# Four changes around the joint of gated mixing, attention and output projection in a one-layer encoder kernel on Trainium2

## The chip, the cores and the metric

The kernel runs on one core of one Trainium2 chip. The metric is the device time of one execution in microseconds (us): the median of three runs. The core has five engines with an instruction queue each: TensorE (PE, matmuls), VectorE (DVE), ScalarE (ACT), GpSimd (POOL) and SyncE (SP), which here issues nearly all DMAs. Each queue is worked off in program order; across engines, semaphores hold an instruction back until its inputs are there and its output buffer is free.

## The reference, cut to what matters

One pre-norm encoder layer on 2048 tokens of width 1024, in float32:

```python
xn = rms_norm(x, mix_norm_g)
q, k, v, f_logit, z = split(xn @ w_in)            # 8 heads of 64; z has 2 x 512 columns
c = cumsum(log_sigmoid(f_logit + b_f))
attn = softmax(causal(q k^T / 8 + c[t] - c[s])) @ v
zu, zv = split(gelu(z)); zv = layer_norm(zv, ln_g, ln_b)
sgu = zu * (masked w_s @ zv + b_s)                # within chunks of 128 tokens, 8 groups of 64
merged = concat(rms_norm(attn, g_a), rms_norm(sgu, g_s))
x = x + merged @ w_out
gate, up = split(rms_norm(x, ffn_norm_g) @ w_gate_up)
x = x + (silu(gate) * up) @ w_down
out = rms_norm(x, final_norm_g)
```

## The kernel before

Every float32 factor is split into a high part in a shorter matmul type and a low part, the rest (names ending in h and l); a product is three matmuls, high by high, high by low, low by high. Making the two parts takes an ACT cast (line 103) and a DVE subtraction (line 108).

The program goes through the input projection (to 356 us of the span), the attention, the output projection (to 1185 us), the up half of the FFN (to 2045 us), the down half (to 2470 us) and a tail. The attention runs 320 steps: for each of 8 heads and each of 4 chunks j of 512 queries, the 4j+4 key blocks of 128 that the mask leaves. A step is two score matmuls into st (lines 627 and 628), an exp by ACT into Pt (line 630), the ACT cast to Ph and the DVE subtraction to Pl, on diagonal blocks two GpSimd selects that put zeros above the diagonal (line 639), and, two steps later, three pv matmuls (lines 646 to 648). After a chunk's last block ACT copies the sums and the denominators out (nd, line 654) and SP stores them (SD, AT); for the last head the denominators of all heads come back as sr, are inverted by DVE, and are stored as RD.

Other work is threaded into the steps by counters on the step number n. The gate path has 8 units of 2 token tiles. A unit is `z_proj` (64 steps of projections, line 696, then copies, a Gelu over 2048 columns on ACT, line 710, the layer norm on DVE with the small power rlr on GpSimd, and the parts zvh and zvl) and `z_mix` (24 small matmuls, line 735; products with DVE, line 740; a sum of squares on ACT, line 746; the power rsr on GpSimd; 8 transposes, line 753; copies sT). The mix of unit i runs inside the projection of unit i+1. The counter goes by n/ZEND, so the gate path is spread over the first 293 steps; projections end at n = 279. From there `out_weights` makes the parts of w_out: 8 loads of 512 KB into two buffers of `xap`, and 16 pairs of a scaled ACT copy (line 835, high part, R0h, R2h, R5h, R6h) and a DVE subtraction (line 836, low part). After its second half has been read, a buffer is loaded again, two loads ahead. At ZEND + 7 the output projection joins the steps: `out_prep` loads a token tile (ST, AT, and the inverse denominators RD), normalises and splits it, line 930 multiplies, and `out_done` stores the sum and the transposed tile XT for the FFN. Token tiles go 0 to 15, FFN halves of 8 tiles in the same order.

The instructions' order on each engine is set by a scheduler that keeps the program's dependencies; it is fixed when the program is built. DMAs on SP are in its order too. Keys (D, C) and values (V) of a head and chunk are loaded two units ahead (`prep`, `load_keys`).

## Time and profile before

| what | us |
|---|---|
| median of three runs | 2479.53 |
| lowest and highest run | 2474.86, 2481.61 |
| the profiled execution | 2481.27 |
| its span, first to last instruction | 2479.6 |
| PE busy | 2415.8 (97%) |
| DVE busy | 1568.5 (63%) |
| ACT busy | 1054.0 (43%) |
| POOL busy | 596.7 (24%) |

All rows below are of the profiled execution, with times from the start of its span. "Busy" of PE is modelled: matmuls are pipelined, so the durations of two that follow each other overlap. The clock that the throttle grants to PE is given as a share of 2.4 GHz.

### The profile page before, as it was taken

What the parts mean: (1) busy time and instruction counts of PE and PEld (TensorE: products, weight loads), DVE (VectorE), ACT (ScalarE), POOL (GpSimd) and SP (SyncE); (2) the same over time, 40 slices, a digit from 0 to 9 for tenths busy, and PEclk for the clock granted to TensorE, in tenths of its full rate; (3) what the DMA queues carried; (4) which work ended last, traced back from release to release, by engine and by line L of the source; (5) the groups of instructions that cost most, each with busy time, mean ns of one, the idle gap of its engine ahead of it and who ended that gap; (6) DMA issues with size and microseconds to landing.
All of it is one profiled execution on the core that took longest, in us unless ns stands there. A gap on an engine that the chain in (4) does not pass through costs nothing. (4 is left out here: it accounts for less than half of the span.)

```text
span 2479.6 us, 31430 instructions
## 1 busy us (share of the span) xinstructions
PE 2415.8 (97%) x10729; PEld 1930.5 (78%) x10729; DVE 1568.5 (63%) x2551; ACT 1054.0 (43%) x1787; POOL 596.7 (24%) x666
## 2 busy tenths in 40 slices
PE   7999999999999989999999999999999999999997
PEld 5777777788787767877888888788888877888876
DVE  4457485666666656466555555875556586696887
ACT  5322226677777776344332322433233242332333
POOL 1000010111111112122232232332323234453441
PEclk9999999999999989999999999999999999999999
DMA  9776565444444337765423223332232244455453
GB/s 312 256 240 199 165 201 144 134 114 127 118 112 115 96 111 194 222 201 166 136 68 94 80 82 94 111 111 77 79 95 74 85 130 168 170 187 192 146 181 144
DMA packets 356263, 355.31 MB, mean 143 GB/s; under 512 B 55364, under 2 KB 276356, under 8 KB 355080
## 3 DMA queue, kind: packets, MB, share of 16 engines
q1 hardware_dynamic: 353800, 344.91, 45.0%
q0 software_dynamic: 2304, 8.39, 1.1%
q8 instruction: 86, 1.41, 0.2%
q14 instruction: 73, 0.60, 0.1%
HBM read 236.50 MB, written 116.72 MB: 142 GB/s over the span
## 5 line engine op out<-in xcount | busy, mean ns | idle before, releaser
L103 ACT CAST wh<-raw 128x512 fp32r<-128x512 f32 (+2 forms) x500 | 309.6, 624 | 796.5 <-PE pp L1300 657.4
L108 DVE TENSOR_TENSOR wl<-raw,wh 128x512 fp32r<-128x512 f32 (+2 forms) x500 | 374.6, 758 | 116.2 <-ACT wh L103 115.8
L1031 POOL TENSOR_TENSOR raw<-raw 128x512 f32<-128x512 f32 (+1 forms) x124 | 165.4, 1335 | 552.5 <-DMA raw<-in_w_gu_dram 365.1
L108 DVE TENSOR_TENSOR Pl<-Pt,Ph 128x512 fp32r<-128x512 f32 (+1 forms) x320 | 194.5, 615 | 158.8 <-ACT Ph L103 155.0
L630 ACT ACTIVATE Pt<-st 128x512 f32<-128x512 f32 (+1 forms) x320 | 167.9, 534 | 149.9 <-PE st L628 148.6
L696 PE MATMUL z<-wh,xz 128*128 128x512 f32 x512 | 199.5, 397 | 0.0
L103 ACT CAST Ph<-Pt 128x512 fp32r<-128x512 f32 (+1 forms) x320 | 176.2, 557 | 22.6 <-PE pv L647 6.2
L1031 DVE TENSOR_TENSOR raw<-raw,raw 128x512 f32<-128x512 f32 (+1 forms) x112 | 133.2, 1191 | 73.2 <-POOL raw L1031 69.3
L337 DVE TENSOR_REDUCE mx<-mx_ps 128x1 f32<-128x512 f32 x192 | 130.8, 686 | 37.6 <-PE mx_ps L335 35.1
L646 PE MATMUL pv<-Ph,V 128*128 128x512 f32 (+2 forms) x320 | 123.6, 387 | 11.7 <-POOL Ph L639 8.8
L639 POOL TENSOR_SCALAR_AFFINE_SELECT Ph<-Ph 128x128 fp32r<-128x128 f32 x128 | 44.2, 345 | 374.7 <-DVE Pl L108 255.0
L627 PE MATMUL st<-A,D 74*128 74x512 f32 (+1 forms) x320 | 120.7, 378 | 3.8 <-ACT Pt L630 3.8
L335 PE MATMUL mx_ps<-D,A 66*128 66x512 f32 (+2 forms) x320 | 118.5, 382 | 4.8 <-DVE mx L337 3.7
L648 PE MATMUL pv<-Pl,V 128*128 128x512 f32 (+1 forms) x320 | 119.7, 375 | 1.0 <-DVE Pl L108 0.4
L628 PE MATMUL st<-B,C 128*128 128x512 f32 (+1 forms) x320 | 118.3, 370 | 0.0
L647 PE MATMUL pv<-Ph,V 128*64 128x512 f32 (+1 forms) x320 | 116.4, 364 | 0.0
L696 PEld LDWEIGHTS z<-wh,xz 128*128 128x128 f32 x512 | 96.7, 189 | 19.2
L1300 PE MATMUL pp<-R2h,wh 128*128 128x512 f32 x264 | 105.4, 399 | 5.7 <-ACT u L1089 5.7
L1300 PE MATMUL pp<-R3h,wl 128*128 128x512 f32 x264 | 105.0, 398 | 2.6 <-DVE wl L108 2.6
L1300 PE MATMUL pp<-R1h,wl 128*128 128x512 f32 x264 | 104.6, 396 | 0.7 <-DVE wl L108 0.7
L1300 PE MATMUL pp<-R2h,wl 128*128 128x512 f32 x264 | 104.9, 397 | 0.2 <-DVE wl L108 0.2
L1146 POOL TENSOR_TENSOR hT<-hT 128x512 f32<-128x512 f32 x44 | 74.4, 1693 | 127.3 <-DVE hT L1145 104.2
(335 smaller groups left out, 6294.1 us busy)
## 6 DMA issues: line engine op xcount, KB each, us to landing
raw<-in_w_gu_dram SPq DMA_DIRECT2D x88, 512.0 KB
HD<-hT SPq DMA_DIRECT2D x44, 512.0 KB
xz<-XS SPq DMA_DIRECT2D x32, 512.0 KB
D<-KH SPq DMA_DIRECT2D x112, 128.0 KB
XA<-xa SPq DMA_DIRECT2D x27, 512.0 KB
xa<-XA SPq DMA_DIRECT2D x24, 512.0 KB
raw<-HD SPq DMA_DIRECT2D x24, 512.0 KB
xb<-XA SPq DMA_DIRECT2D x24, 512.0 KB
```

The lines of the kernel that those rows point to most:

```text
L103: nc.scalar.copy(o, i)
L108: eng.tensor_tensor(o, i, f(h), ALU.subtract)
L335: nc.tensor.matmul(pm[:, 0:n], lhs, Dt[0 : lhs.shape[0], 0:n], start=True, stop=True)
L337: nc.vector.tensor_reduce(mx[:, a, s : s + 1], pm, AX.X, ALU.max)
L627: nc.tensor.matmul(st[:, off:], Dt[:, b * P : (b + 1) * P], A[:, off:], start=True, stop=False)
L628: nc.tensor.matmul(st[:, off:], C[:, b * P : (b + 1) * P], B[:, off:], start=False, stop=True)
L630: nc.scalar.activation(Pt[:, off:], st[:, off:], AF.Exp)
L646: nc.tensor.matmul(pv[:, off:], V[:, 0:P], Ph[:, off:], start=kb == 0, stop=False)
L648: nc.tensor.matmul(pv[:, off:], V[:, 0:P], Pl[:, off:], start=False, stop=kb == 4 * j + 3)
L696: nc.tensor.matmul(pz, xz[:, a, k, :], w[b][:, k, :], start=n == 0, stop=n == 3 * KT - 1)
L1031: (nc.vector if e == "v" else nc.gpsimd).tensor_tensor(o, a, b, op)
L1300: nc.tensor.matmul(pm, a[:, k, :], b[:, k, :], start=on is None and k == 0 and e == 0, stop=k == it.kh - 1 and e == 2, skip_group_check=n ...
```

## The change

There are four edits.

- The last head's query chunks run in the order 3, 2, 1, 0 instead of 0 to 3. Its keys and values, which chunk 3 needs whole, are loaded chunk by chunk, chunk 0 in `prep` and 1 to 3 during head 6's last chunk. The output projection takes the token tiles as 12 to 15, 8 to 11, 4 to 7, 0 to 3, and the FFN takes its second half of tiles first.
- In the gate path, the mix of unit 6 no longer runs inside the projection of unit 7 but behind it, in one piece ("on" makes the step loop take it without a break), and that of unit 7 after it. ZEND goes from 293 to 299, so the projections end at n = 285.
- The high parts of w_out are made by GpSimd (`tensor_scalar_mul`) instead of ACT.
- In the input projection of the last chunk, behind the values of its second token tile, an Exp of 4 columns is added on ACT, ahead of the first exp of the attention, which loads the exp table before.

```diff
-ZEND = 293
+ZEND = 299
...
+        if xc.c == NCH - 1 and tt == 1:
+
+            nc.scalar.activation(T(p1, [P, 4], F32, "r1a"), f(v[:, 0, 0:4]), AF.Exp)
...
-        load_keys(h, j)
+        if h < H - 1 or j == NCH - 1:
+            load_keys(h, j if h < H - 1 else 0)
...
-    units = [(h, j) for h in range(H) for j in range(NCH)]
+
+    units = [(h, j) for h in range(H) for j in (range(NCH) if h < H - 1 else range(NCH - 1, -1, -1))]
+    tiles = [4 * j + t for j in range(NCH - 1, -1, -1) for t in range(4)]
...
-                if n >= 8 and n % 2 == 0:
+                if i < H - 1 and n >= 8 and n % 2 == 0:
                     next(mix, None)
                 yield
             for _ in mix:
-                yield
+                yield "on"
             mix = z_mix(i, *res[0])
...
-            nc.scalar.activation(h_, raw[n][:, i, :], AF.Copy, scale=g)
+            nc.gpsimd.tensor_scalar_mul(h_, raw[n][:, i, :], g)
             nc.vector.scalar_tensor_tensor(l_, raw[n][:, i, :], g, f(h_), ALU.mult, ALU.subtract)
...
-        gens = [out_prep(t, o[t]) for t in range(NB)]
+        gens = [out_prep(tiles[t], o[t]) for t in range(NB)]
...
-                        posts.append(out_done(t, o[t]["x"]))
+                        posts.append(out_done(tiles[t], o[t]["x"]))
...
-                next(zg, None)
+                while next(zg, None) == "on":
+                    pass
...
             pv_of(h, j, kb)
+            if (h, j) == (H - 2, NCH - 1) and kb in (3, 7, 11):
+                load_keys(H - 1, (kb + 1) // 4)
...
-                ld(t, XT[s - 1][i])
+                ld(t, XT[2 - s][i])
...
-    sets = ([[Up(half, fi) for fi in range(NF)] for half in range(2)]
+    sets = ([[Up(half, fi) for fi in range(NF)] for half in (1, 0)]
```

Line numbers behind the added lines go up: line 835 becomes 841, 836 becomes 842, 735 becomes 739, 740 becomes 744, 696 becomes 700, 639 becomes 643, 646 to 648 become 650 to 652.

On PE, behind the last projection matmul into z, the order before was (pv of the last diagonal blocks of a chunk, and the next scores):

```order
L696 MATMUL z_9669<-wh_3191,xz_9495 128x512
L646 MATMUL pv_9528<-Ph_9774,V_882_3326 128x384
L647 MATMUL pv_9528<-Ph_9774,V_882_3326 64x384
L648 MATMUL pv_9528<-Pl_9776,V_882_3326 128x384
L627 MATMUL st_9850<-A_9257,D_9252 128x512
L628 MATMUL st_9850<-B_9260,C_9249 128x512
L646 MATMUL pv_9528<-Ph_9791,V_882_3326 128x256
```

and in the changed kernel it is, up to the first of the 24 mix matmuls of unit 6:

```order
L700 MATMUL z_9712<-wh_3191,xz_9555 128x512
L650 MATMUL pv_9768<-Ph_9820,V_884_3329 128x512
L651 MATMUL pv_9768<-Ph_9820,V_884_3329 64x512
L652 MATMUL pv_9768<-Pl_9822,V_884_3329 128x512
L631 MATMUL st_9874<-A_9244,D_9583 128x512
L632 MATMUL st_9874<-B_9247,C_9580 128x512
L739 MATMUL z_9907<-zvh_9187,wsth_3324 128x128
```

The mix matmuls of unit 6 have moved behind the projections of unit 7, all 24 in one run, and the blocks around them are off the diagonal.

On POOL, at the same place, the order before (selects Ph and Pl of the diagonal blocks, and rlr, the power of the last unit's layer norm) was:

```order
L639 AFFINE_SELECT Pl_9793<-Pl_9793 128x128
L639 AFFINE_SELECT Ph_9808<-Ph_9808 128x128
L639 AFFINE_SELECT Pl_9810<-Pl_9810 128x128
L639 AFFINE_SELECT Ph_9855<-Ph_9855 128x128
L639 AFFINE_SELECT Pl_9857<-Pl_9857 128x128
L154 TENSOR_TENSOR rlr_9874<-rla_9872,mhalf_201 128x2
L639 AFFINE_SELECT Ph_9897<-Ph_9897 128x128
```

and after (R0h, R2h, R5h are high parts of w_out out of the loaded xa; rsr is the power of the mix's norm):

```order
L841 TENSOR_SCALAR R0h_9991<-xa_9872,onc_9868 128x512 x2
L841 TENSOR_SCALAR R2h_10067<-xa_10012,onc_9868 128x512 x2
L154 TENSOR_TENSOR rlr_9896<-rla_9894,mhalf_201 128x2
L841 TENSOR_SCALAR R2h_10067<-xa_10045,onc_9868 128x512 x2
L154 TENSOR_TENSOR rsr_9948<-rsa_9946,mhalf_201 128x2
L643 AFFINE_SELECT Ph_10076<-Ph_10076 128x128
L643 AFFINE_SELECT Pl_10078<-Pl_10078 128x128
L643 AFFINE_SELECT Ph_10097<-Ph_10097 128x128
L643 AFFINE_SELECT Pl_10099<-Pl_10099 128x128
L841 TENSOR_SCALAR R5h_10159<-xa_10090,onc_9868 128x512 x2
L841 TENSOR_SCALAR R5h_10159<-xa_10130,onc_9868 128x512 x2
L643 AFFINE_SELECT Ph_10116<-Ph_10116 128x128
```

The high parts, which POOL did not do before, now stand ahead of rlr and ahead of selects.

On DVE, at the third and fourth pair of loads (low parts R2l, R5l; Pl; products of the mix into sg), before:

```order
L836 SCALAR_TENSOR_TENSOR R2l_10010<-xa_9987,onc_9828,R2h_10009 128x512
L108 TENSOR_TENSOR Pl_10062<-Pt_10058,Ph_10060 128x512
L108 TENSOR_TENSOR Pl_10085<-Pt_10081,Ph_10083 128x384
L662 RECIPROCAL sr_10048<-sr_10048 128x32
L740 SCALAR_TENSOR_TENSOR sg_9884<-z_10002,bsc_3497,zr_9124 128x2x64 x2
L836 SCALAR_TENSOR_TENSOR R5l_10106<-xa_10034,onc_9828,R5h_10105 128x512
L108 TENSOR_TENSOR Pl_10116<-Pt_10112,Ph_10114 128x256
```

and after:

```order
L842 SCALAR_TENSOR_TENSOR R2l_10068<-xa_10045,onc_9868,R2h_10067 128x512
L744 SCALAR_TENSOR_TENSOR sg_9968<-z_9969,bsc_3499,zr_9208 128x2x64 x4
L842 SCALAR_TENSOR_TENSOR R5l_10160<-xa_10090,onc_9868,R5h_10159 128x512 x2
L108 TENSOR_TENSOR Pl_10118<-Pt_10114,Ph_10116 128x256
L744 SCALAR_TENSOR_TENSOR sg_9968<-z_10060,bsc_3499,zr_9208 128x2x64 x4
L108 TENSOR_TENSOR Pl_10139<-Pt_10135,Ph_10137 128x128
L842 SCALAR_TENSOR_TENSOR R5l_10160<-xa_10130,onc_9868,R5h_10159 128x512 x2
```

The products of unit 7's mix stand among the low parts, and each R5l now waits for an R5h made by POOL.

## Rows read from the trace of the kernel before

**Rows 1.** The page, part 1: busy time, share of span, instructions.
```profile
PE 2415.8 (97%) x10729; PEld 1930.5 (78%) x10729; DVE 1568.5 (63%) x2551; ACT 1054.0 (43%) x1787; POOL 596.7 (24%) x666
```

**Rows 2.** Windows: us; busy (x instructions) of PE, PEld, DVE, ACT, POOL; clock, DMA, GB/s.
```profile
896.00:948.50 52.50, 42.25 (x173) 29.78 (x171) 38.22 (x71) 44.82 (x87) 15.30 (x32) 0.84 0.56 161
920.00:930.00 10.00, 7.96 (x40) 5.53 (x39) 7.92 (x17) 9.47 (x23) 3.79 (x9) 1.00 0.51 153
```

**Rows 3.** The same view of two stretches at half clock.
```profile
303.70:307.10 3.40, 3.37 (x8) 2.70 (x9) 2.58 (x6) 2.13 (x4) 0.00 (x0) 0.50 0.14 49
...
901.00:918.10 17.10, 14.38 (x48) 11.72 (x49) 13.94 (x27) 12.98 (x25) 5.41 (x9) 0.50 0.38 108
```

**Rows 4.** Timeline, ACT at the Gelu: start, us, engine, line, op, out<-in [idle before <-releaser].
```profile
896.41 0.73 ACT L835 ACTIVATE R0h<-xa,onc 128x512 fp32r<-128x512 f32 x1
...
897.64 1.28 ACT L710 ACT_TABLE_LOAD   x1
...
898.94 1.91 ACT L710 ACTIVATE zr<-zr 128x2048 f32<-128x2048 f32 x1
```

**Rows 5.** Timeline, PE: a wait at 303.73, then the stretch 895 to 949.
```profile
303.73 0.80 PE L335 MATMUL mx_ps<-D,A 66*128 66x512 f32 x1 [2.64 <-DVE mx L337]
...
895.50 0.40 PE L696 MATMUL z<-wh,xz 128*128 128x512 f32 x1
...
895.73 0.33 PE L646 MATMUL pv<-Ph,V 128*128 128x384 f32 x1
...
902.58 0.80 PE L646 MATMUL pv<-Ph,V 128*128 128x512 f32 x1 [4.39 <-POOL Ph L639]
...
906.65 0.80 PE L627 MATMUL st<-A,D 74*128 74x512 f32 x1 [1.15 <-ACT Pt L630]
...
926.65 1.06 PE L753 MATMUL z<-ident,sg 128*128 128x128 f32 x8
...
946.04 0.32 PE L878 MATMUL mx_ps<-ident,rar 128*128 128x128 f32 x1 [0.60 <-POOL rar L154]
...
948.54 0.50 PE L930 MATMUL oz<-R0h,wh 128*128 128x512 f32 x1 [0.26 <-ACT wh L103]
```

**Rows 6.** Timeline, POOL and DVE, 902 to 907.
```profile
902.23 0.29 POOL L639 TENSOR_SCALAR_AFFINE_SELECT Ph<-Ph 128x128 fp32r<-128x128 f32 x1 [5.46 <-DVE Pl L108]
...
903.86 1.13 POOL L154 TENSOR_TENSOR rlr<-rla,mhalf 128x2 f32<-128x2 f32 x1 [1.09 <-DVE rla L152]
...
906.82 1.38 DVE L108 TENSOR_TENSOR zvl<-zr,zvh 128x512 fp32r<-128x512 f32 x2
...
906.98 0.68 POOL L639 TENSOR_SCALAR_AFFINE_SELECT Ph<-Ph 128x128 fp32r<-128x128 f32 x1 [1.99 <-DVE Pl L108]
```

**Rows 7.** Timeline, SP (DMA issues) and ACT, 909 to 940.
```profile
909.35 0.40 SPq L822 DMA_DIRECT2D xa<-in_w_out_dram  x1
...
913.72 0.72 ACT L835 ACTIVATE R2h<-xa,onc 128x512 fp32r<-128x512 f32 x1
...
931.51 0.24 SPq L655 DMA_DIRECT2D SD<-nd  x1
...
933.44 0.72 ACT L835 ACTIVATE R6h<-xa,onc 128x512 fp32r<-128x512 f32 x1 [0.34 <-DMA xa<-in_w_out_dram]
...
939.39 0.33 SPq L663 DMA_DIRECT2D RD<-sr  x1
```

**Rows 8.** Groups on POOL by form: xcount | busy us, mean ns | idle before.
```profile
L1031 POOL TENSOR_TENSOR raw<-raw 128x512 f32<-128x512 f32 x112 | 151.5, 1354 | 523.0 <-DMA raw<-in_w_gu_dram 365.1 <-DVE wl L108 101.1 <-DMA raw<-HD 26.3
L1031 POOL TENSOR_TENSOR xb<-xb,u 128x512 f32<-128x512 f32 x40 | 76.2, 1916 | 23.0 <-DVE xb L1101 10.5 <-DVE u L1098 8.9 <-issue 3.5
...
L212 POOL MEMSET xl<- 128x1024 f32 x1 | 0.9, 949 | 5.8 <-ACT jk L257 5.8
```

**Rows 9.** Timeline, PE at the start of the attention.
```profile
358.92 0.39 PE L627 MATMUL st<-A,D 74*128 74x256 f32 x1 [1.64 <-ACT Pt L630]
...
364.12 1.15 PE L335 MATMUL mx_ps<-D,A 66*128 66x512 f32 x2 [0.15 <-DMA D<-AUG]
```

## The prediction

> **What bounds the kernel now.** I read the busy shares first: TensorE (PE) is busy 97% of the span [rows 1]. So the time changes only where PE stands still or runs at the lower of its clock levels, and all four edits must be judged at such places. The windows say where: between 896 and 948.5 us, the joint of the last projections of the gate path (line 696), the last attention head and the output projection, PE is busy for 42 us only, while ScalarE (ACT) has 44.8, and 95% in 920 to 930 [rows 2]. In the stretch 901.0 to 918.1 the granted clock is 0.50, which is 1.2 GHz instead of 2.4, for 17.1 us with 14.38 us of PE work in it [rows 3].
>
> The timeline of the joint shows why. The last projection matmul leaves PE at 895.73, when the next pv matmul starts [rows 5]. ACT then copies, takes one w_out part, one exp, loads a table (1.28 us), does the 1.91 us Gelu, and must load the exp table again (1.28 us, alike) [rows 4]. PE's scores run out, and pv waits 4.39 us for the masked Ph, which came from ACT after the Gelu [rows 5]. The clock falls in that wait and comes back only after ACT and the masks have caught up. The first output matmul (line 930) starts at 948.54 [rows 5]. So 895.73 to 948.54, 52.8 us, is the stretch to cost.
>
> What would it take at full clock? A 512-column matmul holds PE for 0.23 us (start 895.50, next start 895.73), 0.2325 as a mean, and 384 and 256 columns go in proportion; eight of 128 columns take 1.06, of which I count 0.107 each, since the last one's end is drawn out [rows 5]. In the order the stretch holds 27 score steps (18 of 512 columns, 3 each of 384, 256, 128; two matmuls each), 28 pv steps (16 and 4 each; three matmuls) and 34 narrow ones: 10.8 + 15.9 + 3.6 = 30.3 us. So 52.8 - 30.3 = 22.5 us are lost there: 7.2 to the clock (half of 14.38), 5.5 to the two waits of 4.39 and 1.15 [rows 5], 3.7 to six shorter ones (0.3 to 0.9, the last at 946.04 [rows 5]), the remaining 6.1 to stalls too short to be named.
>
> **The change part by part.** *The tail of the gate path and the reversed head.* After the change the same stretch, last projection matmul to first output matmul, holds other work: 31 score steps (22 of 512), 30 pv steps (24 of 512), and the mixes of both last units, 48 mix matmuls, 16 transposes, 4 small ones: 12.6 + 19.1 + 7.3 = 39.0 us. PE's total work is unchanged, so work comes in that was done elsewhere at full speed, and the comparison is of losses: the new stretch breaks even at 39.0 + 22.5 = 61.5 us. What it loses:
>
> Gelu gap. The 24 mix matmuls of the unit before (2.6 us) and one 512-wide step fill PE while ACT does copy, table, Gelu, table. ACT no longer has the w_out part and the exp in between (from 896.41 to 897.64, 1.2 us [rows 4]), so rlr, which started 8.1 us after 895.73 (at 903.86, right behind the rla that it reads [rows 6]), could start at 6.9.
>
> The gap comes back through GpSimd (POOL). In the new POOL order the first two R2h operations stand ahead of rlr, the tiny power (1.13 us) that the normalisation waits for. Before, rlr stood behind selects only. R2h needs the third w_out load, which SP issues only when DVE has read the first buffer; before, this load was issued at 909.35 and used at 913.72, so at most 4.4 us to land [rows 7]. With R0l finished some 2.5 us after the last projection, the load is there at 6.9, two R2h end at 8.7, rlr at 9.8 instead of 8.0. Behind it hang two DVE steps and the zvh casts on ACT, and behind those casts, in ACT's order, the Ph cast. PE's stock ends at about 8.3, pv comes at 11.5 to 12, then waits for Pl about 1.6: 5.1 us.
>
> Second gap. The fifth load follows R2l in the same way, at 20 to 21, and lands by 25. Four R5h stand on POOL ahead of two selects, and R5l stands on DVE ahead of four line 744 products that the Square on ACT waits for, and that Square stands ahead of an exp. PE runs dry at about 25 until 28.5 to 29.5, and R6h costs another 1.5 later: 5.5 us.
>
> Small stalls: before, 3.7 + 6.1. ACT gives up 16 operations of 0.73 us like that of 896.41 [rows 4], 10 to 11.7 us (each overlaps the next by up to 0.1), in just the windows where it was at 95% [rows 2]; I take half of the old figure, 4.9. Clock: gaps of this size cost a stretch at half clock. The wait of 2.64 us at 303.73 [rows 5] was followed by 3.4 us at half clock with 3.37 us of PE work, a loss of 1.7 [rows 3]. Two such: 3.0 to 3.4, and I take 3.0.
>
> Sum: 39.0 + 5.1 + 5.5 + 4.9 + 3.0 = 57.5 us, 4.0 below break-even.
>
> *Price of the GpSimd operation.* The trace has no POOL tensor_scalar of 128x512. From below: a memset, which reads nothing, takes 0.95 us for 1024 columns, so 0.47 for 512. From above: the two-input TENSOR_TENSOR of 128x512 takes 1.35, and 1.92 in the form that runs beside much DVE work [rows 8]. The nearest in kind is the one-input select, 0.29 for 128 columns when nothing is beside it [rows 6]; with four times the columns and one fixed part I take 0.9, and use it above. 16 of them are 14 us, on an engine that has 15.3 us of work in 52.5 [rows 2]; it has room, so the price is paid only through the two queues named.
>
> The Trainium skill, GPSIMD Engine Reference, section 3.1, gives 769 ns as measured for 512 elements of a one-input loop; by that estimate the eight operations in the two chains are some 1 us shorter together, which would make the sum 56.5. No run here shows it yet.
>
> *Order of the last head and of the token tiles.* The first output tiles now need head 7's last query chunk, which is done first. Its division chain took 7.9 us from SD at 931.51 to RD at 939.39 in the nearest case [rows 7]; in the new order it starts about 34 us after the last projection and is through by 48, before the first output matmul at 57. No cost. A chunk of 4 key blocks ends the attention, and the tiles go through the output projection and the FFN in an order that is mirrored in both places, with the same loads and stores: nothing. Key loads of the last head go out while head 6 runs, and the 16 DMA engines are used 56% in the stretch [rows 2]: nothing.
>
> *Exp table ahead.* The first exp of the attention loads its table, again 1.28 us, and PE waits 1.64 us for ACT at 358.92 [rows 9]. Loading it earlier removes that wait. But the matmul at 364.12 waited for the load of D from AUG [rows 9], one of a chain of SP issues that starts from the values v; none of those moves. So PE arrives 1.3 us earlier and waits there instead, 0.15 becoming about 1.3. Bounds: 0 and 1.3 + 1.7 (if a half-clock stretch as at 303.7 goes too [rows 3]); I take 0.3.
>
> Total gain 4.3 us. The profiled execution took 2481.27 us (span 2479.6 plus 1.7 outside), the median of the runs 2479.53. Against the former I get 2477.0; against the median, which is what the result is compared with, **2475.2 us**. What this kernel's measurement can tell from no change is about 0.3%, 7.4 us.
>
> **The rivals.**
> *Faster: the chains hide.* For it: PE has no other lack, ACT loses some 10 us of work in its fullest windows, and before the w_out loads were nearly always in time (the one wait for them, at 933.44, is 0.34 [rows 7]). If POOL is ahead of its chains, both gaps shrink to 2 us, with 1.0 for the clock: 39.0 + 4 + 4.9 + 1.0 = 48.9, a gain of 12.6, so 2466.6 with the exp part. Against it: rlr and the selects stand behind R2h and R5h in POOL's fixed order.
>
> *Slower: contention on POOL.* The same select that takes 0.29 us takes 0.68 at 906.98, while DVE runs the two-input zvl from 906.82 on [rows 6]. R2l and R5l are two-input operations, one for each GpSimd operation. At the 1.92 us end of the price, eight operations in the chains cost 8.2 us more and the half-clock stretch stays at its old 17 us (7.2 instead of 3.0): 57.5 + 8.2 + 4.2 = 69.9, a loss of 8.4; with the exp part 2487.6. It decides from 1.4 us an operation on, even with the clock as forecast (8 x 0.5 = 4.0, my whole margin). The Trainium skill, SBUF — State Buffer, section Who interferes with whom, has it that a DVE instruction with two SBUF inputs contends with a GpSimd instruction that reads SBUF. The selects agree, and by that rule this rival is the outcome wherever line 841 on POOL and line 842 on DVE overlap.
>
> *No change: the clock stays down.* The two new gaps are 17 us apart. If PE stays at half clock between them as it did from 901.0 to 918.1, the clock term is 7.2 instead of 3.0 and the stretch takes 61.7: 2479.4. A form of "it doesn't do what it says" is in it: the gap is moved, not filled.
>
> **How the numbers follow.** Forecast 0.48, own range 2470 to 2479 (gaps of 8 to 13 us, price 0.47 to 1.35). Faster rival 0.25, slower rival 0.14, no change 0.13. Faster by over 0.3% is below 2472.1: all of the faster rival and a quarter of the forecast, 0.37. Slower by over 0.3% is above 2486.9: the slower rival, 0.14. The rest, 0.49, is within. The range reaches from 2465 (the faster rival with some margin) to 2486: it leaves out the slower rival and a little below, 0.18.
>
> **What would show it.** In the changed profile: pv waiting 3 to 4 us on ACT about 8 us after the last projection matmul, with POOL's R2h waiting on the w_out load and rlr right behind; a second wait about 17 us later with R5h on POOL and R5l on DVE; a GpSimd operation of 0.9 us; the first output matmul 57 us after the last projection matmul, and two half-clock stretches of 3 to 4 us each or one of 7. At the start, the first exp 1.3 us earlier and the matmul of 364.12 still at 364, waiting on the D load. I am wrong if the first output matmul comes before 52 or after 62 us, if the GpSimd operations take over 1.4 us, or if the output projection or the FFN changes in length by more than 1 us.

## The result and the profile after

The changed kernel took 2488.62 us in the median of 6 runs (2482.73 to 2492.04), the kernel before 2480.57 us in 6 runs beside them. The ratio is 1.0031, 95% interval 1.0020 to 1.0043: slower by 8 us, where I had forecast 2475.2 and a range of 2465 to 2486. The profiled execution took 2492.04 us, with a span of 2489.9; it is the slowest of the six.

The page's busy shares (columns as in [rows 1]) hardly move: PE has 3 us more, ACT 9 less, POOL 25 more.

```profile
PE 2419.1 (97%) x10729; PEld 1932.4 (78%) x10729; DVE 1568.5 (63%) x2551; ACT 1044.6 (42%) x1772; POOL 622.2 (25%) x682
```

The windows (columns as in [rows 2]) show the joint, from the last projection matmul to the first output matmul, and the three stretches at half clock in it:

```profile
900.90:967.50 66.60, 51.58 (x225) 36.25 (x223) 46.75 (x88) 44.27 (x87) 34.85 (x41) 0.85 0.50 143
912.90:923.10 10.20, 8.44 (x21) 5.63 (x22) 8.66 (x18) 8.33 (x17) 3.22 (x3) 0.50 0.01 2
933.40:940.20 6.80, 4.45 (x13) 3.47 (x14) 3.01 (x9) 3.82 (x9) 4.62 (x7) 0.50 0.86 196
...
964.10:967.50 3.40, 3.02 (x11) 1.78 (x9) 2.31 (x6) 1.78 (x4) 2.65 (x6) 0.50 0.92 299
```

A measure that can be read from such rows, and that the rest of this text uses, is a stretch's loss: PE's idle time plus half of its busy time at half clock. Here it is 66.6 - 51.6 = 15.0 idle and (8.44 + 4.45 + 3.02) / 2 = 8.0, together 23.0 us. Before, [rows 2] and [rows 3] give 52.5 - 42.25 = 10.3 and 14.38 / 2 = 7.2, together 17.4 (17.5 when the ends of the stretch are taken to the hundredth, as in the table below). So the joint lost 5.5 us more, and in the joint the prediction had 57.5 us against a break-even of 61.5; it took 66.4 (901.10 to 967.50).

Two waits of PE carry it (timeline, columns as in [rows 5]):

```profile
901.10 0.39 PE L650 MATMUL pv<-Ph,V 128*128 128x512 f32 x1
...
914.10 0.79 PE L650 MATMUL pv<-Ph,V 128*128 128x512 f32 x1 [3.97 <-ACT Ph L103]
...
935.75 0.58 PE L650 MATMUL pv<-Ph,V 128*128 128x256 f32 x1 [5.82 <-POOL Ph L643]
...
967.50 0.77 PE L936 MATMUL oz<-R0h,wh 128*128 128x512 f32 x1
```

They took the place of the 4.39 and 1.15 of [rows 5]. The rows of POOL in the same stretch say what stands behind them:

```profile
907.83 3.13 POOL L841 TENSOR_SCALAR R2h<-xa,onc 128x512 fp32r<-128x512 f32 x2 [8.49 <-DMA xa<-in_w_out_dram]
910.93 0.72 POOL L154 TENSOR_TENSOR rlr<-rla,mhalf 128x2 f32<-128x2 f32 x1
...
929.00 6.19 POOL L841 TENSOR_SCALAR R5h<-xa,onc 128x512 fp32r<-128x512 f32 x4 [1.86 <-DMA xa<-in_w_out_dram]
935.14 0.56 POOL L643 TENSOR_SCALAR_AFFINE_SELECT Ph<-Ph 128x128 fp32r<-128x128 f32 x1
```

POOL waits for the load, makes two R2h in 3.13 us, and only then rlr, which its input would have allowed at 908.1. The zvh cast on ACT waits for what DVE makes with it (zr, line 726), and the Ph cast that PE waits for is the next on ACT. The second time four R5h take 6.19 us and the select of Ph is next in POOL's queue; PE starts 0.05 us after it. On DVE and ACT the same chain shows as the waits for R5h and for the products of the mix:

```profile
912.91 0.62 ACT L103 CAST zvh<-zr 128x512 fp32r<-128x512 f32 x1 [4.28 <-DVE zr L726]
...
930.60 1.17 DVE L842 SCALAR_TENSOR_TENSOR R5l<-xa,onc,R5h 128x512 fp32r<-128x512 f32 x1 [2.82 <-POOL R5h L841]
...
934.72 0.63 ACT L750 ACTIVATE jk<-sg 128x512 f32<-128x512 f32 x1 [5.13 <-DVE sg L744]
```

The price of one operation, by tile (duration min/median/max in ns, first and last start), is in the view of line 841:

```profile
L841 POOL TENSOR_SCALAR R0h<-xa,onc x4: 1559/1570/2074, 892.6 to 897.8; 128x512 fp32r<-128x512 f32 x4
L841 POOL TENSOR_SCALAR R2h<-xa,onc x4: 1557/1578/1778, 907.8 to 913.2; 128x512 fp32r<-128x512 f32 x4
L841 POOL TENSOR_SCALAR R5h<-xa,onc x4: 1561/1562/1571, 929.0 to 933.6; 128x512 fp32r<-128x512 f32 x4
L841 POOL TENSOR_SCALAR R6h<-xa,onc x4: 1562/1897/2364, 939.1 to 945.7; 128x512 fp32r<-128x512 f32 x4
```

It is 1.56 us undisturbed, not 0.9. The rest of the loss lies in the output projection, from the first output matmul to the last transposes of xn. Before and after, in that order:

```profile
948.50:1179.70 231.20, 225.09 (x1053) 180.72 (x1054) 131.22 (x187) 95.96 (x157) 49.12 (x73) 1.00 0.62 192
```

```profile
967.50:1191.00 223.50, 216.38 (x1007) 174.79 (x1008) 124.78 (x178) 83.04 (x136) 47.67 (x75) 0.98 0.63 194
```

Idle is 6.1 before and 7.1 after; half-clock stretches at its end, and after also at its start and at 1056.2, hold 2.5 and 9.2 us of PE work (counted to 1 us past the rows' end), so the losses are 7.3 (6.1 + 2.5/2) and 11.7 (7.1 + 9.2/2). That is 4.4 us where I had put none. Of these, 1.7 are half the PE work of a half-clock stretch at the start (967.5 to 970.9), which begins in the joint. Another stretch stands at a wait of the transposes of xn, which is longer than any of their waits before except the last one (2.8 us, in both kernels):

```profile
1056.40 1.08 PE L903 MATMUL tp<-ident,xn 128*128 128x128 f32 x4 [2.16 <-DVE raa L152]
```

The other stretches differ little: 0.9 more in the input projection, 1.0 more at the start of the attention, 1.4 more in the rest of it up to the last projection, and 0.8 less behind the output projection.

### The profile page after: what moved, and what is told of

Same layout as the page of the kernel before. It is cut to its first block, busy times and chain, and to the rows that moved or that the text cites. A ratio compares the mean times of both kernels' runs of the same rounds, so it can differ in the third digit from the quotient of the medians.

```text
span 2489.9 us, 31441 instructions
## 1 busy us (share of the span) xinstructions
PE 2419.1 (97%) x10729; PEld 1932.4 (78%) x10729; DVE 1568.5 (63%) x2551; ACT 1044.6 (42%) x1772; POOL 622.2 (25%) x682
## 5 line engine op out<-in xcount | busy, mean ns | idle before, releaser
L103 ACT CAST Ph<-Pt 128x512 fp32r<-128x512 f32 (+1 forms) x320 | 175.8, 557 | 26.4 <-PE pv L651 11.7
L650 PE MATMUL pv<-Ph,V 128*128 128x512 f32 (+2 forms) x320 | 123.5, 386 | 14.6 <-POOL Ph L643 10.2
L651 PE MATMUL pv<-Ph,V 128*64 128x512 f32 (+2 forms) x320 | 117.4, 367 | 0.0
L700 PEld LDWEIGHTS z<-wh,xz 128*128 128x128 f32 x512 | 96.9, 189 | 20.8 <-ACT zr L713 1.0
```

The costliest lines, as they stand in the source:

```text
L103: nc.scalar.copy(o, i)
L650: nc.tensor.matmul(pv[:, off:], V[:, 0:P], Ph[:, off:], start=kb == 0, stop=False)
L700: nc.tensor.matmul(pz, xz[:, a, k, :], w[b][:, k, :], start=n == 0, stop=n == 3 * KT - 1)
```

## The experiments

My theory after the result: the time of a GpSimd operation (1.56 us where I took 0.9) sets both waits in the joint, and all else that I put at nothing is small. The rivals: the moved mixes, or the descending order, cost it themselves. The table has every experiment's ratio to the kernel before (run beside it; the experiments came in five batches in which its median was 2477.6 to 2479.4 us, so the column of times doesn't compare across rows) and the losses, worked out as above from PE's busy time and the half-clock stretches, of the joint and of the output projection in the profiled execution. P is the GpSimd high parts, M the moved mixes, D the descending order, X the early exp table; the changed kernel is PMDX.

| run | edits | us | ratio (95%) | joint loss | output loss |
|---|---|---|---|---|---|
| before | none | 2480.57 | 1 | 17.5 | 7.3 |
| changed | PMDX | 2488.62 | 1.0031 (1.0020 to 1.0043) | 23.0 | 11.7 |
| e1_act | MDX | 2480.21 | 1.0012 (1.0003 to 1.0021) | 18.3 | 8.0 |
| e2_pool | P | 2487.24 | 1.0034 (1.0022 to 1.0047) | 29.0 | 5.4 |
| e3_asc | PMX | 2481.58 | 1.0016 (1.0007 to 1.0025) | 22.3 | 6.9 |
| e4_exp | X | 2479.51 | 1.0008 (1.0000 to 1.0017) | 16.9 | 7.8 |
| e5_mixold | PDX | 2488.75 | 1.0050 (1.0037 to 1.0063) | 24.6 | 9.1 |
| e6_dve | MDX, parts by VectorE | 2480.35 | 1.0010 (1.0000 to 1.0021) | 15.8 | 11.2 |
| e7_mix | M | 2478.54 | 1.0006 (0.9997 to 1.0015) | 17.1 | 6.5 |
| e8_desc | D | 2486.07 | 1.0040 (1.0026 to 1.0054) | 21.2 | 12.7 |
| e10_half | MDX, half of P | 2480.89 | 1.0002 (0.9993 to 1.0011) | 17.5 | 7.4 |
| e11_mx | MX | 2480.59 | 1.0005 (0.9996 to 1.0013) | 16.8 | 7.8 |
| e12_descpos | D, x buffers by place | 2484.96 | 1.0021 (1.0013 to 1.0030) | 20.8 | 8.0 |
| e13_mdxpos | MDX, x buffers by place | 2485.02 | 1.0016 (1.0007 to 1.0025) | 18.5 | 11.3 |
| e15_halfonly | half of P | 2483.56 | 1.0018 (1.0009 to 1.0027) | 24.5 | 7.9 |
| e16_r0only | R0h of P | 2477.54 | 1.0002 (0.9993 to 1.0011) | 19.7 | 6.9 |
| e17_descyield | D, product later | 2484.22 | 1.0026 (1.0016 to 1.0037) | 21.1 | 9.1 |
| e18_halfyield | MDX, half of P, product later | 2485.97 | 1.0035 (1.0022 to 1.0048) | 14.6 | 15.1 |
| e20_mr0 | M, R0h of P | 2478.79 | 0.9995 (0.9986 to 1.0004) | 15.4 | 8.7 |
| e21_mdxr0 | MDX, R0h of P | 2477.08 | 0.9996 (0.9987 to 1.0004) | 14.4 | 10.8 |

The losses are of one execution each, and the profiled executions spread as the runs do, so a loss explains a ratio only where both go the same way. Nor is the ratio the quotient of two medians: the two differ by up to 0.11% (the quotient is 1.0029 for e8_desc), so differences of 0.1% between rows carry no weight.

### The GpSimd parts: taken away, alone, in smaller doses, by VectorE

**Taken away (e1_act).**

```diff
-            nc.gpsimd.tensor_scalar_mul(h_, raw[n][:, i, :], g)
+            nc.scalar.activation(h_, raw[n][:, i, :], AF.Copy, scale=g)
```

> The changed kernel with one edit undone: the 16 high parts of w_out are made by ScalarE again. Theory (price of the GpSimd operation): it took 1.56 to 2.4 us in place of my 0.9, and rlr and the selects behind it cost the waits of 3.97 and 5.82 us and the half-clock stretches behind them. Then both waits fall under 2 us, the stretch from the last projection matmul to the first output matmul falls from 66.4 to 56 to 60 us, and the time is 2478 to 2482, no slower than before. Rival (the moved mixes and the reversed order themselves cost it): the stretch stays over 63 us and the time at 2486 to 2490.

The time fell to 2480.21; of the excess of 0.31%, 0.12% is left. In PE's timeline the waits became these:

```profile
908.48 0.50 PE L631 MATMUL st<-A,D 74*128 74x512 f32 x1 [2.45 <-ACT Pt L634]
911.08 0.79 PE L650 MATMUL pv<-Ph,V 128*128 128x512 f32 x1 [1.39 <-ACT Ph L103]
...
927.84 0.58 PE L650 MATMUL pv<-Ph,V 128*128 128x256 f32 x1 [1.70 <-POOL Ph L643]
```

The wait of 5.82 is now 1.70, and the joint's loss 18.3 in place of 23.0. The stretch took 62.7 us, longer than the 56 to 60 I expected, and the interval of the ratio lies above 1, so "no slower than before" was wrong: with the parts on ScalarE the filled Gelu wait comes back as 2.45 us on ACT. The output projection's loss fell too, from 11.7 to 8.0, which the theory does not explain.

**Alone (e2_pool).** The same line changed in the kernel before.

> The kernel before with this edit alone: the 16 high parts of w_out by GpSimd, all else as before. Theory (price of the GpSimd operation): 16 operations of 1.56 us in front of selects and rlr, in a stretch with diagonal blocks; the stretch 52.8 us grows by 5 to 10, the time is 2485 to 2491. Rival (it costs only together with the new order): ScalarE is freed of 10 us, the stretch shrinks by 2 to 5, the time is 2475 to 2479.

2487.24, in the middle of what the theory gave. POOL, then PE:

```profile
908.73 5.34 POOL L835 TENSOR_SCALAR R2h<-xa,onc 128x512 fp32r<-128x512 f32 x3
914.04 0.29 POOL L639 TENSOR_SCALAR_AFFINE_SELECT Ph<-Ph 128x128 fp32r<-128x128 f32 x1
```

```profile
914.38 0.79 PE L646 MATMUL pv<-Ph,V 128*128 128x512 f32 x1 [8.02 <-POOL Ph L639]
```

Three R2h stand ahead of a select, and PE waits 8.02 us for it. The joint's loss is 29.0, and the stretch grew by 11.8 us, a little more than the 5 to 10 expected. So the edit by itself costs what the whole change costs.

**Smaller doses.** Half: of each loaded pair the first part by GpSimd, the second by ScalarE, in the changed kernel (e10_half) and in the kernel before (e15_halfonly):

```diff
+            if i:
+                nc.scalar.activation(h_, raw[n][:, i, :], AF.Copy, scale=g)
+            else:
+                nc.gpsimd.tensor_scalar_mul(h_, raw[n][:, i, :], g)
```

> The changed kernel with half the dose: of each loaded pair of high parts, the first by GpSimd, the second by ScalarE, 8 operations each. Theory (GpSimd's price, paid in the queue ahead of rlr and the selects): each GpSimd group shrinks from 3.1 or 6.2 us to half, the waits of 3.97 and 5.82 us to 2 to 4, and the time lies between all on ScalarE (2480.2) and all on GpSimd (2488.6): 2482 to 2486. Rival (the price is one of contention that starts with any GpSimd operation): 2486 to 2489.

> The kernel before with half a dose: of each loaded pair of w_out high parts the first by GpSimd, the second by ScalarE; all else as before. All 16 by GpSimd cost 0.34% here. Theory (queue of 1.56 us operations ahead of rlr and the selects): the long wait of 8.02 us falls to about half, and the time is 2478 to 2483. Rival (any GpSimd part ahead of a select costs the same, since one wait for a load is enough): 2484 to 2488.

In the changed kernel half the dose costs nothing that can be measured (1.0002), better than I expected. Only one R2h now stands ahead of rlr, and the long waits are 2.01 and 3.28, with one of 1.85 for ACT ahead of the first:

```profile
907.94 1.57 POOL L844 TENSOR_SCALAR R2h<-xa,onc 128x512 fp32r<-128x512 f32 x1 [11.60 <-DMA xa<-in_w_out_dram]
909.89 1.15 POOL L154 TENSOR_TENSOR rlr<-rla,mhalf 128x2 f32<-128x2 f32 x1 [0.38 <-DVE rla L152]
```

```profile
910.50 0.50 PE L631 MATMUL st<-A,D 74*128 74x512 f32 x1 [1.85 <-ACT Pt L634]
...
913.72 0.80 PE L650 MATMUL pv<-Ph,V 128*128 128x512 f32 x1 [2.01 <-ACT Ph L103]
...
931.34 0.58 PE L650 MATMUL pv<-Ph,V 128*128 128x256 f32 x1 [3.28 <-POOL Ph L643]
```

rlr waits for rla again, not for POOL. The first gap is only a little shorter for it (1.85 + 2.01, against 0.59 + 3.97 with all 16); the second is. In the kernel before, half the dose costs 0.18%, half of the 0.34% of the full one, with a median (2483.56) just above what I expected: the wait of 8.02 fell to 4.70, but one of 3.94 stands ahead of it at 903.15. The smallest dose, R0h alone (`if n > 1` in place of `if i`):

> The kernel before with only the first four high parts (R0h, whose data are loaded long before) by GpSimd, so that no GpSimd operation waits for a load, and rlr has none of them right ahead of it if they run during the last projections. Theory: ScalarE is freed of 4 operations around the Gelu and no wait is added: 2475 to 2480, at best 3 us faster than before. Rival: in the order before, R0h runs after the last projection (897.4 to 903.0 with all 16), so selects still wait: 2480 to 2485.

1.0002: no cost, and no gain either, though ScalarE has four operations less. Doses of 4, 8 and 16 in the kernel before cost 0.02, 0.18 and 0.34%. The rival's fear was right in the trace: there is a wait of 3.23 us at 901.48 for ACT and one of 4.62 at 908.89 behind a select, and the joint's loss is 19.7; but in the time this doesn't show.

**By VectorE (e6_dve).** `nc.vector.tensor_scalar_mul` in the same place of the changed kernel.

> The changed kernel with the high parts by VectorE instead of GpSimd. Its one-input operations of 128x512 took 0.44 to 0.47 us in the mix (line 750 before). Theory (the price of the operation on GpSimd is what costs, not the wait for the load): nothing of 1.56 us stands before selects or rlr, the two long waits shrink to under 2.5 us and the time is 2476 to 2481, at or below that with ScalarE (2480.2). Rival (the loads that follow the low parts are the cause): waits of 3 to 5 us remain, 2484 to 2489.

```profile
L841 DVE TENSOR_SCALAR R0h<-xa,onc x4: 478/479/482, 900.3 to 903.8; 128x512 fp32r<-128x512 f32 x4
L841 DVE TENSOR_SCALAR R2h<-xa,onc x4: 473/500/521, 918.6 to 924.6; 128x512 fp32r<-128x512 f32 x4
```

The same operation takes 0.48 us there, and the loads follow the low parts as before. The longest wait in the joint is 1.22 us and the loss 15.8, against 23.0. So it is the operations' time in GpSimd's queue and not the loads. (A cheaper operation in the same queue, which would part its price from its place, was not run; half the dose is the nearest to it.) The output projection lost 11.2 in this run, and the time stayed at 1.0010.

### The moved mixes and the exp table

**Mixes undone in the changed kernel (e5_mixold):** ZEND 293, `n >= 8` for every unit, no "on".

> The changed kernel with the moved mixes alone undone (ZEND 293, unit 6's mix inside the projections of unit 7). Theory (GpSimd's price bounds the joint): the high parts by GpSimd stand as before in front of rlr and selects, with nothing of PE's to cover them: 2486 to 2492, as the GpSimd edit alone. Rival (the moved mixes are part of the loss): 2482 to 2486.

1.0050, the slowest of all, though its interval and that of the changed kernel just overlap. The waits are 3.23, 4.25 and 3.28 us, which fits the theory that the GpSimd chains have less to hide behind. The moved mixes are no part of the loss.

**Mixes alone (e7_mix), and with the exp table (e11_mx).**

> The kernel before with the moved mixes alone (unit 6's mix behind the projections of unit 7, in one piece; ZEND 299), high parts on ScalarE, ascending order, no early exp table. Theory: 24 mix matmuls fill the wait for the Gelu (4.39 us) and the half-clock stretch of 17.1 us goes or shrinks to 7, so the time falls by 2 to 6 us: 2472 to 2476. Rival (what is put behind the projections only lengthens the part that ScalarE bounds; the run without GpSimd parts still had waits of 2.45, 1.39 and 1.70 us): within 2 us of before, 2476.5 to 2481.

> The changed kernel with two edits undone, the GpSimd high parts and the descending order; what is left is the moved mixes and the early exp table. Each alone was within 0.1% of before. Theory (they add up): 2478 to 2482. Rival (the moved mixes need the off-diagonal blocks of the descending order around them): 2482 to 2485.

Both are within what can be told from no change, as the rival of the first and the theory of the second had it. The wait for the Gelu is filled, as I said, but another one comes on ACT a little later, in e7_mix (3.05 us) as in e11_mx:

```profile
908.65 0.69 PE L630 MATMUL st<-A,D 74*128 74x384 f32 x1 [3.06 <-ACT Pt L633]
910.65 0.80 PE L649 MATMUL pv<-Ph,V 128*128 128x512 f32 x1 [0.99 <-ACT Ph L103]
914.31 0.79 PE L649 MATMUL pv<-Ph,V 128*128 128x512 f32 x1 [1.15 <-DVE rsa L152]
```

**Exp table alone (e4_exp).**

> The kernel before with the early load of the exp table alone. Theory of the prediction: TensorE's wait for the first exp falls from 1.64 to under 0.5 us, but the matmul at 364 still waits for the load of D, so the gain is 0 to 1 us: 2479.5 to 2480.6. Rival: the whole load counts and a half-clock stretch goes with it, gain 1.5 to 3 us: 2477.5 to 2479. Second rival: the changed schedule of the input projection loses as much as in the changed kernel (0.9 us): 2481 to 2482.

No gain (1.0008). PE's timeline, and the window behind it:

```profile
357.41 0.39 PE L630 MATMUL st<-A,D 74*128 74x256 f32 x1 [0.33 <-ACT Pt L633]
...
363.53 0.70 PE L335 MATMUL mx_ps<-D,A 66*128 66x512 f32 x2 [2.05 <-DMA D<-AUG]
```

```profile
365.40:372.20 6.80, 6.80 (x18) 5.24 (x18) 4.47 (x7) 2.59 (x5) 0.00 (x0) 0.50 0.74 205
```

The wait of 1.64 in [rows 9] fell to 0.33, and the 0.15 of the matmul that waits for D became 2.05. A half-clock stretch follows it with 6.8 us of PE work, where 3.3 us of work stood at half clock before.

### The descending order

**Undone in the changed kernel (e3_asc), and alone in the kernel before (e8_desc).** The edits are those of the change, from `units` to `sets`.

> The changed kernel with the order of the last head's chunks, of the token tiles and of the FFN halves undone (ascending again). Theory (price of the GpSimd operation): the waits behind GpSimd remain, also behind diagonal blocks that come sooner; 2485 to 2492. Rival (the descending order costs the output projection, whose own losses grew from 3.3 to 7.7 us): 2481 to 2485, with the losses from the first output matmul to the FFN back at 3 to 4 us.

> The kernel before with the descending order alone (last head's chunks, token tiles, FFN halves). Prediction's theory: no cost, 2476.5 to 2480. Rival, from the run with the ascending order put back, which was 0.15% nearer to before than the changed kernel: the descending order costs 2 to 5 us by itself, 2480 to 2484, lost between the first output matmul and the FFN, where the last tiles' normalisation then has attention steps of short blocks beside it.

Undone, the time comes to 1.0016 in place of 1.0031 (the intervals overlap a little), with an output loss of 6.9 where before has 7.3: the rival's number. (The 3.3 and 7.7 of the expectation are 4.0 lower than this text's 7.3 and 11.7, with the same difference.) Alone, it costs 0.40%, as much as the GpSimd parts, and more than the rival of e8_desc had. That is the second cost that I had put at nothing. Both stretches lose: the joint 21.2, where 3.1 of the 3.7 more are half-clock stretches (10.3 against 7.2) and only 0.6 idle time, and the output projection 12.7. In the latter:

```profile
1012.54 1.09 PE L899 MATMUL tp<-ident,xn 128*128 128x128 f32 x4 [3.01 <-DVE raa L152]
1053.73 0.63 PE L899 MATMUL tp<-ident,xn 128*128 128x128 f32 x4 [1.02 <-DVE raa L152]
```

```profile
1009.69 0.69 DVE L864 TENSOR_TENSOR raw<-raw,rd 128x512 f32<-128x512 f32 x1 [5.95 <-DMA raw<-AT]
```

DVE's product of the next tile waits 5.95 us for its load and stands ahead of the product xn that the transposes need. Before, the longest such wait was 2.90.

**Two attempts on that cause.** By number, the one buffer xb goes to tile 14 and then to tile 8, two places on; `x_tile(pos)` gives it to every third place again (e12_descpos; with ScalarE's parts and the other edits, e13_mdxpos). And one more `yield` between a tile's loads and its product (e17_descyield; e18_halfyield in the changed kernel with half the GpSimd parts):

```diff
-        o["x"] = x_tile(t)
+        o["x"] = x_tile(pos)
...
         yield
+        yield
         nc.vector.tensor_tensor(r[:, 0:4, :], r[:, 0:4, :], rd, ALU.mult)
```

> The descending order alone, as in the run that was 0.40% slower than before, with one thing mended: the buffer of x for a token tile goes by its place in the new order, not by its number, so that the one xb buffer comes every third tile again (by number it is tile 14's and then tile 8's, two places on). Theory (the reuse distance of the x buffers): the waits of 3.01 and 1.02 us in the output projection go, and the time falls by 3 to 6 us to 2478 to 2482. Rival (the three denominator chains that now stand in SP's queue among the tile loads): 2484 to 2487, waits as they were.

> The descending order alone (2486.1, x buffers by number as there), with the product of a token tile with its inverse denominators put one place later in the program behind its loads. Theory (this product waits up to 5.95 us for its load and stands ahead of the xn product on VectorE, for which the transposes wait 3.01): the transposes' waits at 1012 and 1053 fall under 1 us, the losses from the first output matmul on fall from 12.7 to 8 to 9 us, and the time is 2480 to 2483. Rival (x buffers only): waits and time as they were, 2484 to 2488.

> The changed kernel with high parts on ScalarE (2480.2) and the x buffers by place in the order. Theory (reuse distance): the remaining wait of 0.7 us at 1049 goes and little else, as the moved mixes shift the tiles: 2477 to 2480. Rival: no difference, 2479 to 2482.

> The changed kernel with half the high parts on ScalarE (2480.9, equal to before) and the product of a token tile one place later behind its loads. Theory: the wait of 0.70 us at 1048 goes, a gain of 0 to 2 us: 2477.5 to 2481. Rival (a later product delays the tile's normalisation and output matmuls wait): 2482 to 2486.

With the buffers by place the descending order costs 0.21% instead of 0.40, but the intervals overlap, and by the medians it is 5.6 us above before instead of 7.3; the wait of 3.01 is 1.38, that of 1.02 is gone, and the output loss is 8.0. The time, 2484.96, is the rival's and not the 2478 to 2482 that I expected. With the later product the two waits are gone (none over 0.3 at these transposes) and the output loss is 9.1, as expected, but a wait on ACT's wh cast (1.57 at 1040) stands in their place, the ratio is 1.0026, and the time, 2484.22, is again the rival's. In the changed kernel neither helps. Buffers by place brought an output loss of 11.3 and 1.0016, against 1.0012 without (e1_act), with a time above both forecasts. The later product brought 15.1 and 1.0035, against 1.0002 without (e10_half): there it costs, since the two intervals don't meet, as its rival had it. So the output projection's loss goes up and down with the whole schedule by 4 to 8 us, and neither piece settles the descending order's cost. What is shown is that it costs, and that waits of this kind stand in its trace; how much of the cost they are is not shown, nor what brings the half-clock stretches in the joint.

The runs also show that the costs don't add. Without the moved mixes the GpSimd parts cost 0.34%, the descending order 0.40%, both together 0.50% (e5_mixold, with the exp table). With the moved mixes and the exp table (1.0005), the GpSimd parts bring it to 1.0016, the descending order to 1.0012, and both to 1.0031. So the mixes, which gain nothing alone, take back, with the exp table beside them, most of what the descending order costs by itself (1.0040 to 1.0012, the intervals far apart).

### Is there a version that beats both?

> The kernel before with the moved mixes and with R0h alone by GpSimd (4 of 16 operations). R0h should run before the last projection matmul, as in the changed kernel (892.6 to 897.8), ahead of no rlr. Theory (ScalarE freed of 4 operations at the Gelu, no wait added): 1 to 3 us better than the moved mixes alone (2478.5): 2475 to 2478, faster than before. Rival: the Gelu wait is set by the two table loads and the Gelu, so nothing moves: 2478 to 2481.

> The changed kernel with only R0h by GpSimd and the other 12 high parts on ScalarE. Theory (the cost is in the groups that wait for loads ahead of rlr and of selects): as with all on ScalarE or better, 2477 to 2481, against 2488.6 with all 16. Rival (the descending order's waits in the output projection come back by a shift of the schedule): 2482 to 2486.

With only R0h by GpSimd, on data that were loaded long before, the joint loses 15.4 us (e20_mr0) and 14.4 (e21_mdxr0), less than before. In the latter the four operations run from 891.7 to 898.4, ahead of the last projection matmul; in the former, against what I expected, they run from 895.7 to 902.6 and end some 5 us behind it. The times are 0.9995 and 0.9996 of before, with intervals that hold 1. Against the changed kernel's 1.0031 both are 0.35% better; neither can be told from the kernel before, and for e20_mr0 that is what the rival had.

## Why the prediction was wrong, point by point

**What bounds the kernel, and where.** Right: nothing outside the joint and the neighbouring output projection moved by more than 1.5 us.

**The joint's two chains.** Right in mechanism and place: rlr behind two R2h (forecast 11.5 to 12 us after the last projection matmul for pv, measured 914.10 - 901.10 = 13.0, wait 3.97), and R5h ahead of a select and R5l ahead of the mix's products (forecast to end at 28.5 to 29.5, measured 935.75 - 901.10 = 34.7, wait 5.82). The first came 1.0 to 1.5 us late, about what two operations of 1.56 take longer than two of 0.9 (1.3). The second came 5 to 6 us late: four operations took 2.6 longer, and the load ahead of them was there only 27.9 us after the last projection matmul (929.00 - 901.10), where I had 25.

**The price of the GpSimd operation.** This is the first step that failed. I had 0.47 and 1.35 to 1.92 as ends and took 0.9 by the one-input select, extrapolated with a guess at its fixed part; the measured 1.56 lies above the two-input TENSOR_TENSOR of the same size (1.35 in [rows 8]). Scaling the select by columns alone would have given 4 x 0.29 = 1.16, and the point from which I said that the sign turns was 1.4. With 1.56 in my own sum, eight operations cost 8 x 0.66 = 5.3 us more and the joint comes to 62.8, past the break-even of 61.5. With the 16 operations out of GpSimd's queue, the joint's idle time falls from 15.0 us to 11.0 (e1_act) and 7.3 (e6_dve). The Trainium skill (GPSIMD Engine Reference, section 3.1) has 769 ns for 512 elements as the best case of a loop; this trace shows twice that for this operation.

**The clock and the small stalls.** Here the sum failed too. I had 3.0 us for two short stretches; the rows give 8.0 in three. The same term is 7.3 in e1_act, 8.6 in e6_dve and 7.0 in e10_half, so among these kernels, which differ only in who makes the high parts, it doesn't go with the price on GpSimd, and e6_dve has it with no wait over 1.3 us. With 8.0 in place of 3.0, and nothing else changed, the sum is 62.5, past the break-even as well.

Term by term, the 66.4 us are 39.0 of work, 11.3 in the two gaps (3.97 and 0.56; 5.82 and, for R6h, 0.93), 8.0 of clock, and 8.1 that are left for the small stalls. I had 10.6, 3.0 and 4.9. So the gaps were nearly as long as forecast although the price was not 0.9, and that is luck. Their ends came late, but PE also ran dry late, 9.0 and 28.8 us after the last projection matmul (914.10 - 3.97 and 935.75 - 5.82), where I had 8.3 and 25. The half-clock stretch between them, with 8.44 us of PE work, put off the second by some 4 us (an estimate, half of 8.44). The small stalls, which I had halved because ACT gives up some 10 us of work, stayed near their old 9.8; what keeps them up was not taken apart.

**The rivals.** The slower one came true in result (2487.6 forecast, 2488.62 measured) but not by its mechanism. The operation needs 1.56 without anything beside it, and the six that stand ahead of the two waits took 1.56 to 1.59 each, two of the R5h with R5l running inside them. It was R5l that grew there, to 1.17 us where line 836 took 0.75 before. On GpSimd five others of the 16 grew, to between 1.72 and 2.36, and in e2_pool two of the three R2h ahead of the select did (1.71 and 2.10). The rule that a two-input VectorE operation and a GpSimd read disturb each other (Trainium skill, SBUF — State Buffer, section Who interferes with whom) agrees with these rows in kind; that the slower rival is the outcome wherever lines 841 and 842 overlap, as I had put it, does not hold for R5h. Its figure was met by luck: it had nothing for the output projection. The faster rival failed, since the gaps didn't shrink. The rival in which the clock stays down had the clock's cost nearly right (7.2, measured 8.0), though the clock was back at full between 923.1 and 933.4; it had nothing for the stalls.

**The order of the last head and of the tiles.** Wrong, and the other step that failed: put at nothing, it costs 0.40% alone, and undoing it takes 0.15 of the changed kernel's 0.31%. The output projection, where I had no loss, lost 4.4 us more. I had argued from the lead of the denominator chain and from equal counts of loads, and not from which DVE product would stand ahead of which, or from the x buffers by tile number.

**The exp table.** Right: the wait moved to the load of D, and the gain is none (forecast 0.3 us). I had not seen that the new wait would lengthen a half-clock stretch.

**The moved mixes.** Right that they fill the Gelu wait; wrong that this shows in the time. Alone they change nothing, since the next thing that is late is ACT, a few us on. They do take back part of what the other edits cost: without them the same change is at 1.0050 instead of 1.0031, and the descending order at 1.0040 instead of 1.0012 (there with the exp table).

## What to carry to other kernels

When work moves to an engine with spare time, its price is paid by what is queued behind it there: look for the small operations (a reciprocal square root, a mask) that others wait for, and take for the price the dearest near form in the trace, not one stretched from a smaller shape. Move only the pieces whose data lie ready and that have no such operation behind them; in the kernel before, four of sixteen cost nothing, eight half of the loss, sixteen all, and in the changed kernel neither four nor eight cost anything that shows. Take the cost of a clock stretch from the largest case in the trace that is like yours, not from the shortest: here that term alone turned the sign of the sum. A change of order with equal work is not free: read which operation comes ahead of which on each in-order engine, and which buffers turn by number.

## What the runs showed of the hardware

A scaled copy of 128x512 from float32 to the matmul's type takes 1.56 us on GpSimd, 0.72 on ScalarE and 0.48 on VectorE. With VectorE work beside it the GpSimd one grew to between 1.72 and 2.36 us in five of 16 cases; in two others it kept to 1.56, and the two-input VectorE operation beside it grew from 0.75 to 1.17. In all 20 kernels there were stretches at half clock in the joint, and they cost PE between 4.4 and 11.0 us (half of its busy time in them).
